# Releasing the steps of a woven encoder kernel by an in-kernel model of engine and tile times instead of fixed pauses

## The chip, the cores and the metric

The kernel runs on one core of one Trainium2 chip. Its time is the device time of one execution, in microseconds (us). Three runs of the kernel before gave 2302.92 to 2304.68 us, median 2303.62 us. The profiled execution has a time of its own, given with the profile below.

The engines have these names in the profile: PE is TensorE's matmul stream and PEld its weight loads, DVE is VectorE, ACT is ScalarE, POOL is GpSimd, SP is SyncE, whose queue issues most DMAs here.

## What is computed

The reference is one inference step of a two-layer encoder for 1024 prompt frames and 32 sample frames, with a model width of 1024. Layer 0 mixes with a matrix memory (mLSTM), layer 1 with sliding-window attention. Each is followed by a SwiGLU block, and each sub-layer ends in a layer norm of `alpha * x + sublayer(x)`:

```python
def layer_norm(x, g, b):
    mu = jnp.mean(xf, -1, keepdims=True)
    var = jnp.mean(jnp.square(xf - mu), -1, keepdims=True)
    return (xf - mu) * lax.rsqrt(var + LN_EPS) * g + b

def swiglu(x, w_gu, w_down):                  # D_FF = 2816
    g, u = jnp.split(x @ w_gu, 2, axis=-1)
    return (jax.nn.silu(g) * u) @ w_down

# mLSTM, per chunk and head; C is the matrix memory, n its normaliser
num = w_inter[..., None] * (q @ C0) + (q @ k.T * d) @ v
den = w_inter * (q @ n0) + sum(q @ k.T * d, -1)
h = num / jnp.maximum(jnp.abs(den), jnp.exp(-m))[..., None]
C_new = decay * C0 + einsum('bhs,bhsd,bhse->bhde', w_end, k, v)

# attention with a sink, 16 query heads on 2 shared key/value heads of 64
s = q @ k.T * HEAD_DIM ** -0.5 + bias         # own chunk of 64 and the two before
p = exp(s - mx) / (sum(exp(s - mx), -1) + exp(sink - mx))
o = p @ v

for layer in range(2):                        # trunk
    x = layer_norm(alpha * x + mixer[layer](x))
    x = layer_norm(alpha * x + swiglu(x))
```

It is done once for the prompt and once for the sample, and it also returns the updated memory states and the last keys and values.

## The kernel before, in words

The 1056 frames are the columns of every product; the 1024 features lie on partitions as 8 tiles of 128. Columns are worked in three groups (`GRP`: 384, 384, 288) or four quarters of 264.

**Dense products.** Every fp32 product is three matmuls on fp32r parts: high by high, high by low, low by high. `gemm` (L346) issues them as lines L358, L359, L360. A *low half* is the difference between a value and its rounded high half. It is one subtraction on DVE or POOL after a cast on ACT: for weights L198 and L200 (`wr` is the raw tile, `wh` and `wl` its halves, `ex` and `oh` halves kept elsewhere), for activations L388 and L389, in a layer norm L460 and L466, for attention weights L1627 and L1628.

**SwiGLU.** The blocks use a seven-product scheme of sums of blocks (banks `A` and `B`). The hidden values are staged to DRAM by `stage` and its `put` (L1139 cast, L1140 low half, then a store to `hs_*`) and loaded again by `feed` and `load`.

**The order of work around the change.** The program is one list that Python writes; each engine runs its own part of it in order, and semaphores hold an instruction whose inputs are late. What is not dense work is written as generators ("tasks"): the layer norm (`ln_task`), the matrix memory, attention, the staging, the reloads. `Weave.tick(us)` is called after each three matmuls of `gemm` with their nominal time; it counts down every task's pause, and a task whose pause is over writes its next instructions and yields the next pause. So the pauses (`GAP_M`, `GAP_A`, `LN_PACE`, `RUSH`, `FEED_W` 1.7, `FEED` 2.0, 5.2 in `stage`) fix how many dense matmuls lie on PE between two steps of a task. `pipeline` drives the items of the matrix memory (36: 4 head pairs by 9 chunks of 128 or 32 frames) and of attention (72: 8 head pairs by 9 chunks) through stages with a lag of an item between them. Which engine takes a low half is fixed: `on_vector` for weights, alternation elsewhere.

**A matrix memory item** is: scores `S` (L846), the mask product `p` on DVE (L850), values `H` (L862, L864) and the new state `T` (L867), a norm in small DVE and ACT steps (`small`, from L873), `ht` (L906), two transposes `T` (L913), a copy to `act` (L915).

**An attention item** is: scores of two heads `psS` (L1580, L1581), a fused bias and minimum on DVE (L1586), exp on ACT (L1598), a reciprocal on DVE (L1602), two scalings by it on POOL (L1604), four transposes `T` (L1624), high half on ACT and low half on DVE (L1627, L1628), values `O` (L1639, L1640), a copy and two additions to `act` (L1648, L1650).

**A layer norm of a quarter** is: two statistics matmuls `ln` (L418), four differences and squares, sums of squares (L427), two more statistics matmuls (L432), scale (ACT, DVE), and per pair of tiles a multiplication, ACT scalings, a high half (L460) and a low half (L466).

## Time and profile before

| what | value |
|---|---|
| runs, median (lowest, highest) | 2303.62 us (2302.92, 2304.68) |
| profiled execution, span | 2307.5 us |
| PE busy | 2222.9 us, 96% |
| DVE, ACT, POOL busy | 1462.9, 1024.3, 1127.6 us |
| granted TensorE clock, mean | 0.989 |

The span is from the first to the last instruction of one execution, here 3.9 us longer than the median of the runs. The stages, in time: projections to about 100 us; matrix memory between projections to 360; output projection and first layer norm to 640; SwiGLU of layer 0 to 1150 and its norm to 1250; attention between dense projections to 1510, with the output projection from about 1445; its layer norm to 1640; SwiGLU of layer 1 to 2215; the last norm and the stores to 2307.5.

In the tables of windows below, a row is: start and end in us, length, then busy time and number of instructions of PE, PEld, DVE, ACT and POOL, the granted clock, the busy share of the DMA engines and what they moved in GB/s. A row of waits is: engine, output and line that waited, what it waited for, us in total, times, longest. A row of a group is: line, engine, operation, output and inputs with shapes, count, busy us, mean ns of one, then idle time before it with what ended it.

### The profile page before, as it was taken

What the parts mean: (1) busy time and instruction counts of PE and PEld (TensorE: products, weight loads), DVE (VectorE), ACT (ScalarE), POOL (GpSimd) and SP (SyncE); (2) the same over time, 40 slices, a digit from 0 to 9 for tenths busy, and PEclk for the clock granted to TensorE, in tenths of its full rate; (3) what the DMA queues carried; (4) which work ended last, traced back from release to release, by engine and by line L of the source; (5) the groups of instructions that cost most, each with busy time, mean ns of one, the idle gap of its engine ahead of it and who ended that gap; (6) DMA issues with size and microseconds to landing.
All of it is one profiled execution on the core that took longest, in us unless ns stands there. A gap on an engine that the chain in (4) does not pass through costs nothing.

```text
span 2307.5 us, 44305 instructions
## 1 busy us (share of the span) xinstructions
PE 2222.9 (96%) x17224; PEld 2171.8 (94%) x17224; DVE 1462.9 (63%) x2754; ACT 1024.3 (44%) x2300; POOL 1127.6 (49%) x1039
## 2 busy tenths in 40 slices
PE   8999999999999999999999899899999999999997
PEld 8889989999999999999998799889999999999997
DVE  4354466768666655466667677767666666456657
ACT  3343445446444444322247687746444444431124
POOL 2443332125666666454314576723766666554422
PEclk9999999999999999999999999999999999999999
DMA  4221111401443434697423110331334444398712
GB/s 144 66 58 54 53 41 47 140 19 61 144 159 140 145 138 150 210 315 248 157 79 127 52 54 21 108 115 46 99 139 149 156 150 147 115 332 268 239 60 76
DMA packets 165089, 289.71 MB, mean 126 GB/s; under 512 B 15824, under 2 KB 120840, under 8 KB 164880
## 3 DMA queue, kind: packets, MB, share of 16 engines
q1 hardware_dynamic: 160528, 282.56, 36.3%
q10 hardware_dynamic: 4352, 4.33, 0.5%
q8 instruction: 135, 2.21, 0.4%
q14 instruction: 74, 0.61, 0.1%
HBM read 203.89 MB, written 82.94 MB: 124 GB/s over the span
## 4 chain that ended last, share of the span: by engine, by line
PE 75%; DVE 9%; ACT 7%; DMA 4%; issue 3%; POOL 2%; SPq 0%; DVEq 0%; ACTq 0%; POOLq 0%
PE A L358 9%; PE A L359 9%; PE A L360 9%; PE d L358 8%; PE d L360 7%; PE d L359 7%; PE B L358 7%; PE B L359 7%; PE B L360 7%; ACT act L454 1%; PE T L1624 1%; DMA wr<-in_dn 1%; DVE z L592 1%; POOL s L1604 1%; ACT sx L460 1%
## 5 line engine op out<-in xcount | busy, mean ns | idle before, releaser
L200 POOL TENSOR_TENSOR wl_s<-wr,wh_s 128x512 fp32r<-128x512 f32 x224 | 316.2, 1432 | 241.5 <-ACT wh_s L198 177.4
L358 PE MATMUL d<-sx,wh 128*128 128x264 f32 (+2 forms) x1080 | 349.2, 323 | 8.9 <-ACT sx L388 8.9
L359 PE MATMUL d<-sx,wh 128*128 128x264 f32 (+2 forms) x1080 | 334.2, 309 | 4.4 <-POOL sx L466 3.4
L360 PE MATMUL d<-sx,wl 128*128 128x264 f32 (+2 forms) x1080 | 334.0, 309 | 3.7 <-DVE wl L200 2.9
L198 ACT CAST wh_s<-wr 128x512 fp32r<-128x512 f32 x224 | 135.5, 617 | 320.9 <-DVE wr L175 288.7
L358 PE MATMUL A<-sx,wh_s 128*128 128x264 f32 x896 | 254.6, 284 | 2.2 <-ACT z L1268 2.2
L359 PE MATMUL A<-sx,wh_s 128*128 128x264 f32 x896 | 254.2, 284 | 0.0
L360 PE MATMUL A<-sx,wl_s 128*128 128x264 f32 x896 | 254.0, 283 | 0.0
L200 POOL TENSOR_TENSOR wl<-wr,wh 128x512 fp32r<-128x512 f32 (+2 forms) x106 | 143.8, 1365 | 219.8 <-ACT wh L198 206.2
L358 PEld LDWEIGHTS d<-sx,wh 128*128 128x128 f32 x1080 | 208.8, 193 | 13.5 <-ACT sx L388 9.4
L359 PEld LDWEIGHTS d<-sx,wh 128*128 128x128 f32 x1080 | 208.6, 193 | 6.7 <-POOL sx L466 4.2
L360 PEld LDWEIGHTS d<-sx,wl 128*128 128x128 f32 x1080 | 207.9, 192 | 4.7 <-DVE wl L200 3.4
L200 POOL TENSOR_TENSOR wl_a<-wr,wh_a 128x512 fp32r<-128x512 f32 x112 | 170.4, 1528 | 52.0 <-ACT wh_a L198 43.0
L358 PE MATMUL d<-sx,ex 128*128 128x264 f32 x624 | 181.5, 291 | 4.4 <-DVE act L1067 4.4
L360 PE MATMUL d<-sx,ex 128*128 128x264 f32 x624 | 178.3, 286 | 3.0 <-DVE ex L200 3.0
L359 PE MATMUL d<-sx,ex 128*128 128x264 f32 x624 | 177.7, 285 | 0.0
L358 PEld LDWEIGHTS A<-sx,wh_s 128*128 128x128 f32 x896 | 168.4, 188 | 2.7 <-ACT z L1268 2.7
L360 PEld LDWEIGHTS A<-sx,wl_s 128*128 128x128 f32 x896 | 168.8, 188 | 0.0
L359 PEld LDWEIGHTS A<-sx,wh_s 128*128 128x128 f32 x896 | 168.4, 188 | 0.0
L1140 POOL TENSOR_TENSOR z<-z 128x528 fp32r<-128x528 f32 x76 | 105.0, 1382 | 104.0 <-issue 51.5
L1604 POOL TENSOR_SCALAR s<-s,st 128x256 f32<-128x256 f32 (+1 forms) x144 | 122.4, 862 | 50.4 <-DVE st L1602 30.7
L1139 ACT CAST z<-z 128x528 fp32r<-128x528 f32 x136 | 85.9, 631 | 94.7 <-DVE z L1152 47.4
(322 smaller groups left out, 7375.9 us busy)
## 6 DMA issues: line engine op xcount, KB each, us to landing
wr<-in_gu SPq DMA_DIRECT2D x96, 512.0 KB, 4.5
hs_x<-z SPq DMA_DIRECT2D x72, 528.0 KB, 2.8
hs_t<-z SPq DMA_DIRECT2D x64, 528.0 KB, 3.5
sx<-hs_x SPq DMA_DIRECT2D x112, 264.0 KB, 5.2
sx<-hs_t SPq DMA_DIRECT2D x64, 264.0 KB, 5.8
ex<-hs_t SPq DMA_DIRECT2D x64, 264.0 KB, 6.6
wr<-in_dn SPq DMA_DIRECT2D x32, 512.0 KB, 6.4
ex<-hs_x SPq DMA_DIRECT2D x32, 264.0 KB, 5.7
```

The source lines that it names most:

```text
L198: self.nc.scalar.copy(hi, r)
L200: eng.tensor_sub(lo, r, hi.bitcast(F32))
L358: nc.tensor.matmul(out, ah, bh, start=start and k == 0, stop=False, **kw)
L359: nc.tensor.matmul(out, ah, bl, start=False, stop=False, **kw)
L360: nc.tensor.matmul(out, al, bh, start=False, stop=stop and k == last, **kw)
L454: nc.scalar.activation(z, z, AF.Identity, scale=gk, bias=bk)
L460: nc.scalar.copy(s2(0, kk), z2(kk))
L592: nc.vector.tensor_add(acc, acc if i > 3 else pair[1], pair[0])
L1139: nc.scalar.copy(hi.bitcast(F32R), buf(s))
L1140: eng.tensor_sub(lo.bitcast(F32R), buf(s), hi)
L1604: nc.gpsimd.tensor_scalar_mul(p[:R, h, lo:256], p[:R, h, lo:256], st[:R, 2, h : h + 1])
L1624: nc.tensor.transpose(pt[:nk, i, h, :R], p[:R, h, c : c + nk], ident[:R, :R])
```

## The change

`GAP_M`, `GAP_A`, `FEED_W`, `FEED`, `LN_PACE`, `RUSH` and `pipeline` go. A class `Clock` sees every instruction as it is written and keeps, while Python writes the program, a modelled time for each engine, for each cell of each tile, for the DMA pipe, for a lock between DVE and POOL, and for a halved TensorE clock after windows with little matmul work. A step of a task is an `At`: its engine, what it reads and writes, the buffers it needs. `Weave.tick` writes each step whose modelled start lies no later than PE's modelled time plus a lead (0.45 us; for PE steps minus 0.2 us). `Clock.sooner` gives a subtraction or addition to whichever of DVE and POOL the model ends first; it decides for weights prepared ahead (L392), `split_act`, sums, products and low halves of the layer norm (L658, L697), the staging (L1376) and the sums for the second product (L1436). `Weights.feed` becomes a task. Matrix memory and attention are written as one generator per item, and the scores of attention are released head by head. The arithmetic is the same.

```diff
+class Clock:
...
+    def begin(self, e, at):
+        held = self.lock if self.holder != e else 0.0
+        return max(self.free[e], at, held)
+
+    def sooner(self, n, *reads):
+        at = self.time(reads)
+        cost = {"DVE": 0.155 + 0.00104 * n, "Pool": 0.17 + 0.00219 * n}
+        e = min(cost, key=lambda e: self.begin(e, at) + cost[e])
+        return {"DVE": self.nc.vector, "Pool": self.nc.gpsimd}[e]
...
+            self.slow = self.window < 0 or self.busy < self.QUIET / 2
...
 class Weave:
...
-    def tick(self, us):
-        if self.feed:
-            self.feed(us)
-        for t in list(self.tasks):
-            t[1] -= us
-            while t in self.tasks and t[1] <= 0.0:
-                self._step(t)
+    def tick(self, until=0.0):
+        moved = True
+        while moved:
+            moved = False
+            for t in list(self.tasks):
+                while t in self.tasks:
+                    at = self._start(t)
+                    now = max(self.clk.now, until)
+                    if at is None or at > now + self.LEAD.get(self._engine(t), 0.45):
+                        break
+                    self._step(t)
+                    moved = True
...
         self.nc.scalar.copy(hi, r)
-        eng = self.nc.vector if key in self.on_vector else self.nc.gpsimd
+        if self.ahead:
+            eng = self.clk.sooner(w, hi)
+        else:
+            eng = self.nc.vector if key in self.on_vector else self.nc.gpsimd
         eng.tensor_sub(lo, r, hi.bitcast(F32))
...
-        us = 3 * (max(out.shape[-1], 256) / 2400.0 + 0.003)
+        wv.tick(clk.time((lhs[0][0], rhs[0][0]), (out,)))
         for k, ((ah, al), (bh, bl)) in enumerate(zip(lhs, rhs)):
...
-            wv.tick(us)
+            wv.tick()
...
             kk = s - 3
             if kk >= 0 and not final:
-                eng = nc.gpsimd if kk & 1 else nc.vector
-                eng.tensor_sub(s2(1, kk), z2(kk), s2(0, kk).bitcast(F32))
-            yield y[6]
+                yield At("EITHER", [s2(0, kk)], [s2(1, kk)])
+                clk.sooner(2 * w, s2(0, kk)).tensor_sub(s2(1, kk), z2(kk), s2(0, kk).bitcast(F32))
...
+    def attend(n, j, b):
...
+        for h in range(2):
+            yield At("Pool", [p[:R, h, lo:256], st[:R, 2]])
+            nc.gpsimd.tensor_scalar_mul(p[:R, h, lo:256], p[:R, h, lo:256], st[:R, 2, h : h + 1])
+        yield At("PE", [p[:R, :, lo:256]], room=[ring(psb, "T", 2)])
+        pt = new(psb, "T", [P, 2, 2, P], bufs=2, hold=True)
...
+        yield At("PE", lambda: [low[:], VR[:, [vi for _, _, vi in kts][-1]]], room=[ring(psb, "O", 2)], when=lambda: ast["v"] > b)
+        po = new(psb, "O", [P, 2, P], bufs=2, hold=True)
```

The order of the instructions on an engine, at three places. First PE in the matrix memory, before; `S` reads an item's keys, and the number in `p_2180` and `ht_2340` tells which item's product a row takes, the lower the earlier:

```order
L846 MATMUL S_2291<-qz_215,kT_738 128x256
L848 MATMUL T_2293<-ident,kT_738 128x128
L358 MATMUL d_2260<-wh_0_1920,sx 128x256
L359 MATMUL d_2260<-wl_0_1921,sx 128x256
L360 MATMUL d_2260<-wh_0_1920,sx 128x256
...
L862 MATMUL H_2316<-vt_739,p_2180 128x129
L864 MATMUL H_2316<-Cn_2221,qwz_217 128x129
L862 MATMUL H_2316<-vt_739,p_2180 128x129
L864 MATMUL H_2316<-Cn_2221,qwz_217 128x129
L867 MATMUL T_2317<-vt_739,ks_2182 64x129 x2
```

The change at the same kind of place, from one item's scores to its values and on to the transposes of its result:

```order
L1075 MATMUL S_2157<-qz_214,kT_740 128x256
L1077 MATMUL T_2159<-ident,kT_740 128x128
L582 MATMUL d_2140<-sx,wh_1022 128x384
L583 MATMUL d_2140<-sx,wh_1022 128x384
L584 MATMUL d_2140<-sx,wl_1023 128x384
...
L1098 MATMUL H_2179<-vt_741,p_2155 128x129
L1100 MATMUL H_2179<-Cn_2105,qwz_217 128x129
L1098 MATMUL H_2179<-vt_741,p_2155 128x129
L1100 MATMUL H_2179<-Cn_2105,qwz_217 128x129
L1102 MATMUL T_2180<-vt_741,ks_2156 64x129 x2
```

Before, the values that follow an item's scores belong to the item before it, so some 70 rows lie between the scores and the values that read them; in the change the item's own values come after six dense matmuls.

Second PE at the end of attention, before; `d` is the output projection, `T` the transposes and `O` the values of the last two items:

```order
L358 MATMUL d_17540<-sx,wh_1_17424 128x264
L359 MATMUL d_17540<-sx,wh_1_17424 128x264
L360 MATMUL d_17540<-sx,wl_1_17425 128x264
L1639 MATMUL O_17625<-hi_17583,VR 128x256
L1640 MATMUL O_17625<-lo_17584,VR 128x256
L1639 MATMUL O_17625<-hi_17583,VR 128x256
L1640 MATMUL O_17625<-lo_17584,VR 128x256
L358 MATMUL d_17643<-sx,wh_0_17430 128x264
L359 MATMUL d_17643<-sx,wh_0_17430 128x264
L360 MATMUL d_17643<-sx,wl_0_17431 128x264
L1639 MATMUL O_17651<-hi_17609,VR 128x2x32
L1640 MATMUL O_17651<-lo_17610,VR 128x2x32
```

The same place in the change:

```order
L1837 MATMUL psS_13972<-KH_13974,Q_17004 32x160
L1838 MATMUL psS_13972<-KL_13976,Q_17004 32x160
L1856 MATMUL T_17730<-ident,s_17692 128x128 x4
L1856 MATMUL T_17738<-ident,s_17710 128x32 x2
L1856 MATMUL T_17738<-ident,s_17710 32x32 x2
L1872 MATMUL O_17751<-hi_17736,VR 128x256
L1873 MATMUL O_17751<-lo_17743,VR 128x256
L1872 MATMUL O_17751<-hi_17736,VR 128x256
L1873 MATMUL O_17751<-lo_17743,VR 128x256
L1872 MATMUL O_17756<-hi_17745,VR 128x2x32
L1873 MATMUL O_17756<-lo_17748,VR 128x2x32
```

Before, dense rows stand between the steps of the last items; in the change the last scores, transposes and values follow each other with no dense row between.

Third POOL in the first layer norm, before; `z` is a sum of squares, `sx` a low half of the norm's result, `wl` one of the next weights:

```order
L427 TENSOR_TENSOR z_4632<-z_4632 128x2x264
L466 TENSOR_TENSOR sx<-act,sx 128x2x264 x2
L427 TENSOR_TENSOR z_4632<-z_4632 128x2x264
L466 TENSOR_TENSOR sx<-act,sx 128x2x264 x2
L200 TENSOR_TENSOR wl_0_5723<-wr_4964,wh_0_5722 128x512
L427 TENSOR_TENSOR z_4632<-z_4632 128x2x264
L200 TENSOR_TENSOR wl_0_5782<-wr_5021,wh_0_5781 128x512
L466 TENSOR_TENSOR sx<-act,sx 128x2x264 x2
```

The change:

```order
L658 TENSOR_TENSOR z_4632<-z_4632 128x2x264
L697 TENSOR_TENSOR sx<-act,sx 128x2x264
L658 TENSOR_TENSOR z_4632<-z_4632 128x2x264
L697 TENSOR_TENSOR sx<-act,sx 128x2x264
L392 TENSOR_TENSOR wl_6550<-wr_6316,wh_6549 128x512
L392 TENSOR_TENSOR wl_6555<-wr_6316,wh_6554 128x512
```

Fewer low halves of the norm stay on POOL; the others are on DVE. Over the whole program the count of instructions is the same on PE, and 247 subtractions and additions of two tiles move from POOL (761, now 514) to DVE (1827, now 2074): 122 low halves of weights, 76 of the staging, 22 of the layer norms, 16 of the sums for the second product, 10 sums of squares and one other.

867 lines of the change are left out of this document (521 added, 346 removed).

## The prediction

> **What bounds the kernel now.** I read the page first, then the clock of the core, then windows by stage, then PE's waits stage by stage.
>
> ```profile
> span 2307.5 us, 44305 instructions
> PE 2222.9 (96%) x17224; PEld 2171.8 (94%) x17224; DVE 1462.9 (63%) x2754; ACT 1024.3 (44%) x2300; POOL 1127.6 (49%) x1039
> core 0: 2307.5 us, clock 0.989
> ```
>
> PE is the bound: 96% of the span. The matmuls stay the same, so the change can win only what PE loses: 2307.5 - 2222.9 = 84.6 us idle, and (1 - 0.989) x 2307.5 = 25.4 us to a lower clock, which hides inside the busy time. The stages share this as follows.
>
> ```profile
> 0.00:100.00 100.00, 90.05 (x586) 86.11 (x587) 37.85 (x79) 37.56 (x86) 26.17 (x46) 0.95 0.31 105
> 100.00:360.00 260.00, 249.49 (x1783) 227.28 (x1783) 139.69 (x542) 108.90 (x387) 104.24 (x201) 0.99 0.19 54
> 360.00:640.00 280.00, 269.85 (x2074) 267.19 (x2073) 192.17 (x276) 139.94 (x266) 109.41 (x76) 0.99 0.25 85
> 640.00:1150.00 510.00, 507.54 (x4167) 507.14 (x4166) 313.33 (x380) 176.68 (x315) 285.62 (x205) 1.00 0.55 187
> 1150.00:1250.00 100.00, 97.30 (x698) 94.59 (x697) 71.54 (x120) 53.38 (x101) 25.40 (x22) 1.00 0.29 95
> 1250.00:1445.00 195.00, 180.67 (x1272) 170.66 (x1270) 145.30 (x554) 148.39 (x458) 133.08 (x166) 0.98 0.18 54
> 1445.00:1510.00 65.00, 54.56 (x396) 51.21 (x395) 52.70 (x146) 45.09 (x125) 45.29 (x43) 0.92 0.42 143
> 1510.00:1640.00 130.00, 123.18 (x966) 120.87 (x965) 92.12 (x131) 73.07 (x131) 49.02 (x33) 0.99 0.17 57
> 1640.00:2215.00 575.00, 572.16 (x4707) 571.55 (x4706) 358.98 (x426) 207.45 (x371) 330.20 (x236) 1.00 0.53 180
> 2215.00:2307.50 92.50, 78.11 (x597) 75.16 (x595) 59.25 (x105) 33.88 (x63) 19.15 (x17) 0.96 0.19 65
> ```
>
> Length less PE busy gives, in this order, 10.0, 10.5, 10.2, 2.5, 2.7, 14.3, 10.4, 6.8, 2.8 and 14.4 us. Both SwiGLU blocks, 1085 us, lose 5.3 us together: nothing can be won there. The 24.3 us before the first products and in the last stores hang on the first loads, the last norm and the stores. What can be won lies in five stages with 10.5 + 10.2 + 2.7 + 24.7 + 6.8 = 54.9 us. PE's waits say for what (the first row of the whole run, then single stages: 100 to 360, 360 to 640, 1250 to 1445, 1445 to 1510):
>
> ```profile
> PE d L358 <- ACT sx L388: 8.9, 3, 5.9
> ...
> PE T L913 <- DVE small L873: 3.1, 2, 1.9
> PE T L867 <- DVE act L915: 2.3, 4, 1.0
> PE T L913 <- DVE ks L853: 2.0, 2, 1.5
> PE S L846 <- DVE p L850: 1.9, 1, 1.9
> PE T L913 <- DVE ht L906: 1.1, 1, 1.1
> ...
> PE d L358 <- DVE act L1067: 4.4, 1, 4.4
> PE d L359 <- POOL sx L466: 1.7, 1, 1.7
> PE d L360 <- DVE wl L200: 1.5, 1, 1.5
> ...
> PE psS L1580 <- DVE st L1586: 5.5, 3, 3.1
> PE psS L1580 <- DVE Q L1498: 2.6, 3, 1.3
> ...
> PE T L1624 <- DVE st L1602: 2.7, 2, 1.5
> PE ln L418 <- DVE z L592: 2.2, 1, 2.2
> ```
>
> These are few waits, one to four each, not one per item: a step released too early stands in PE's queue with ready dense work behind it. A pause that is right for most items is wrong for some, which is what a release by a modelled time addresses.
>
> **The change, part by part.**
>
> *Matrix memory (100 to 360).* Its five rows of waits add to 10.4 us, all that PE loses there. Each is a task's step that came too early. In the change I counted dense rows between a step and its reader: some 70 rows lie between scores and their values before, six at the place shown now. With the durations of these rows the mean cover falls from 7.8 to 4.1 us for scores to values and from 8.5 to 7.3 us for values to transposes (estimates from the order). The new covers are shorter, but each is set where the model says that the input is ready. I leave 2 us: -8.
>
> *Output projection and first norm (360 to 640).* The wait of 4.4 us is behind a DMA: one load of x, ahead of four weight loads on SP's queue.
>
> ```profile
> 402.82 0.59 SPq L1041 DMA_DIRECT2D act<-in_x  x1
> 403.58 14.64 SPq L157 DMA_DIRECT2D wr<-in_wout_a  x4
> ```
>
> The order on SP is the same in the change, but the four loads are written some 7 us of PE's work later, no longer right behind x, and by the order and their 3 to 4 us each they land at least 4 us before PE reads them (estimates); so the wait of 4.4 us should go. The low halves of the norm on POOL are the second reason:
>
> ```profile
> L466 POOL TENSOR_TENSOR sx<-act,sx 128x528 fp32r<-128x528 f32 x24 | 32.8, 1369 | 116.9 <-ACT sx L460 115.7 <-PE d L359 0.7 <-DMA scrx<-act 0.4
> L1271 DVE TENSOR_TENSOR z<-z,B 128x528 f32<-128x528 f32 x40 | 28.1, 702 | 74.0 <-PE B L360 74.0
> ```
>
> 22 of the 24 move to DVE; a subtraction of the same size takes 1369 ns on POOL and about 702 ns on DVE, 0.67 us less on the way to the next product. Of the 10.2 us I leave 3: -7. The same answer at the second norm (6.8 us, same two kinds of wait) is -4, and -1.5 for 1150 to 1250 with the SwiGLU blocks.
>
> *Attention (1250 to 1445).* 31 of the 38 weight low halves that POOL does here move to DVE.
>
> ```profile
> L1604 POOL TENSOR_SCALAR s<-s,st 128x256 f32<-128x256 f32 x112 | 102.2, 925 | 42.8 <-DVE st L1602 27.9 <-PE psS L1581 7.8 <-PE T L1624 3.5
> L200 POOL TENSOR_TENSOR wl<-wr,wh 128x512 fp32r<-128x512 f32 x38 | 49.7, 1317 | 23.0 <-ACT wh L198 20.2 <-PE O L1639 2.1 <-PE d L359 0.7
> L1627 ACT CAST hi<-T 128x512 fp32r<-128x512 f32 x56 | 32.9, 587 | 27.6 <-PE T L1624 27.0
> L1628 DVE TENSOR_TENSOR lo<-T,hi 128x512 fp32r<-128x512 f32 x56 | 38.7, 691 | 12.2 <-ACT hi L1627 11.1
> ```
>
> POOL's scalings no longer stand behind a 1317 ns subtraction. DVE pays 31 x 0.69 = 21 us: its 145.3 + 52.7 = 198 us of 260 become 219, against 235 us of PE. So DVE has room on the mean, but little, and every item passes through it several times. Mean cover from the second scores to the transposes rises from 6.1 to 7.2 us, and from transposes to values falls from 3.6 to 2.4 us, where the two halves alone need 0.59 + 0.69 = 1.3 us. Steady stretches of this stage already lose little, its start a lot:
>
> ```profile
> 1290.00:1315.00 25.00, 21.19 (x133) 19.57 (x133) 16.55 (x61) 16.80 (x52) 15.59 (x18) 0.93 0.27 81
> 1390.00:1415.00 25.00, 24.59 (x179) 23.65 (x179) 20.03 (x78) 19.53 (x62) 17.70 (x23) 1.00 0.12 34
> ```
>
> The waits of 14.3 us are most of them for scores behind the reduction of another head (5.5) and for queries (2.6), which the release by head answers: -8.
>
> *End of attention (1445 to 1510).* Here the change writes the last scores, transposes and values without dense rows between. An item's way from scores to values is a reduction, an exponential, two scalings of 0.93 us, transposes and two halves; I estimate 5.5 to 6 us, and the last two items with the split of their outputs come to 13 to 15 us, of which some 5 us are covered by the rows left. 8.5 to 10 us stay idle, as now 10.4: -1.
>
> *Start and last norm.* No row there hangs on a release: 0. The sum of idle time is -8 - 7 - 4 - 1.5 - 8 - 1 = -29.5 us.
>
> *Clock.* The clock falls to half after a stretch of 3.41 us in which PE was partly idle:
>
> ```profile
> 1481.72:1485.13 3.41, 1.79 (x14) 1.49 (x12) 2.61 (x11) 3.36 (x10) 2.29 (x3) 1.00 0.00 0
> 1485.13:1488.54 3.41, 3.08 (x14) 2.98 (x14) 2.69 (x8) 2.26 (x8) 3.41 (x4) 0.50 0.45 121
> 420.17:423.59 3.42, 0.00 (x0) 0.00 (x0) 3.42 (x6) 3.42 (x9) 1.46 (x1) 1.00 0.27 74
> ```
>
> A half-clock stretch costs about 1.5 us of matmul time. I count 13 outside the last stores, most of the 25.4 us above. If the waits above go, I expect some 6 of them to go: -9. The Trainium skill, page "TensorE: Matmul & The Clock Gate", section "What's actually happening", says that the gate closes after at least one idle window of about 3.4 us. The first row disagrees, since PE was busy for 1.79 of 3.41 us before the half clock. By the page only the stall at 420 would count, whose half-clock stretch is the one or two that go: -3 in place of -9.
>
> *New waits.* A release set by a model has no slack: a step comes when its input should be ready, and any error of the model is a wait on PE. No row of before shows this. From below: the steady stretch above loses 0.41 us in 25, 0.016 us per us; over the 520 us of the matrix memory and attention that is 9 us. From above: the bad stretch loses 3.81 us in 25, 0.152, that is 79 us. I take 10, by the steady stretch, since most items have covers of some us.
>
> The net is -29.5 - 9 + 10 = -28.5 us, a span of 2279.0. The profiled execution is 3.9 us above the median, so the time is 2275.
>
> **The rivals.**
>
> *The model is late in each step.* Attention writes four PE steps per item, two scores, transposes, values, 288 in all. If the model thinks inputs ready 0.25 us too early on the mean, behind a DVE that is busy for 219 of 235 us, PE waits 288 x 0.25 = 72 us. For it speaks the cover of 2.4 us from transposes to values, on queues with low halves of 0.69 us ahead; against it the longer cover of scores. It decides from 28.5 / 288 = 0.10 us a step. Time: 2275 + 72 - 18 (the attention gain and the clock that would not be won) is about 2329; with half that error 2300 or so.
>
> *The waits only move.* Each wait that goes lets PE reach the next one sooner, as at the end of attention, and the clock stays: -29.5 + 28 gives 2302, no change. For it speaks that 10.4 us there stay by my own count; against it that the waits elsewhere are few and unlike each other.
>
> *Nearly all goes.* If the named waits, about 55 us of the five stages, and the 13 half-clock stretches, 20 us, all fall but for some 10 us: 2307.5 - 65, less 3.9, gives 2239. Against it the shorter covers and the end of attention.
>
> *The model does nothing more than the pauses*: the order on each engine differs in most rows, so this is excluded.
>
> **How the numbers follow.** The forecast has 0.57, its own range 2254 to 2293 by the ends of the clock and of the new waits near to it. The late model has 0.14, waits that move 0.14, nearly all gone 0.15. The time is 2275. For 8 in 10 the low end is 2240, at the rival of nearly all, the high end 2306, just above no change; the late model lies outside for the most part. About 0.2%, 4.6 us, is what a measurement can tell: faster is below 2299.0. The forecast and nearly all gone give 0.72, and 0.04 of the waits that move: faster 0.76. Same takes 0.08 of the latter and 0.01 of the late model: 0.09. Slower is 0.02 and 0.13: 0.15.
>
> **What would show it right or wrong.** Right: PE idle in 100 to 360 near 2 us and no row for `small`, `ks` or `ht` above 0.5 us; the wait for `act` after the load of x gone; the wait of scores for the reduction gone; idle time of some 9 us still at the end of attention, ahead of the last values; a mean clock of 0.993 or more. Wrong: waits for `lo` or `hi` ahead of the values in dozens; DVE's low halves of weights named as what ended PE's waits; idle time in the SwiGLU blocks above 8 us, from staging that moved to DVE. If PE's idle time is unchanged and only its places differ, the waits have moved.

## The result and the profile after

The change is slower. Its median is 2326.1 us (four runs, 2324.07 to 2327.41); runs of the kernel before taken beside it have the median 2303.49 us (2302.92 to 2304.68). The ratio is 1.0098, with the interval 1.0084 to 1.0113: 22.6 us lost where 28.6 had been forecast as won, and above the range, which ended at 2306. The ratios and intervals leave out disturbed executions; the profiled one of `mem_dma` below was such a one, so its stages are not read.

The head of the page and the clock of the core, of the change:

```profile
span 2325.6 us, 44258 instructions
PE 2239.0 (96%) x17224; PEld 2182.8 (94%) x17224; DVE 1519.5 (65%) x3001; ACT 1030.2 (44%) x2300; POOL 793.7 (34%) x792
core 0: 2325.6 us, clock 0.980
```

The span grew by 18.1 us. PE has the same 17224 instructions and is 16.1 us longer busy; its idle time is 86.6 us against 84.6. So by the page the loss is in the clock: (1 - 0.980) x 2325.6 = 46.5 us against 25.4. But that holds for the sum only, and the sum hides stages that go opposite ways. To see them I took PE's rows one by one: the interval from each to the next, less the usual interval of rows of the same kind and shape (the 40th percentile of those outside stretches of half clock). Summed over a stage this is what the stage loses, to idle time and to the clock together. The work without loss is the same 2133.5 us in every kernel here, so the columns can be compared. How the rows are grouped moves the level (by 8 us in the sum, with another grouping), but the differences between the columns by no more than about 0.5 us.

| lost, us | before | change |
|---|---|---|
| start to the first matrix memory values | 18.3 | 12.3 |
| matrix memory | 31.6 | 42.9 |
| output projection, first norm | 14.7 | 4.6 |
| SwiGLU of layer 0 | 8.2 | 6.4 |
| its norm, to the first scores | 8.0 | 4.6 |
| attention, to its last values | 46.8 | 85.1 |
| rest of the output projection, norm | 16.5 | 6.6 |
| SwiGLU of layer 1 | 6.1 | 7.3 |
| last norm | 6.5 | 2.2 |
| sum | 156.6 | 171.9 |

Five stages win 33.7 us together (6.0 + 10.1 + 3.4 + 9.9 + 4.3) and the SwiGLU blocks change by less than 2 us each; matrix memory loses 11.3 us more and attention 38.3. After PE's last row 2.5 us more pass. The windows of three stages show it; the columns are as before. Before, matrix memory, the output projection with the first norm, and attention:

```profile
95.00:347.50 252.50, 241.99 (x1746) 219.82 (x1744) 132.53 (x530) 105.01 (x377) 105.38 (x202) 0.99 0.20 56
347.50:567.10 219.60, 210.55 (x1562) 208.06 (x1563) 153.67 (x239) 114.06 (x221) 65.37 (x44) 0.99 0.21 69
1252.90:1491.20 238.30, 216.48 (x1537) 204.18 (x1537) 180.80 (x671) 181.33 (x555) 167.12 (x200) 0.97 0.19 58
```

The same stages of the change:

```profile
95.00:337.10 242.10, 223.64 (x1596) 200.16 (x1594) 124.12 (x531) 97.72 (x359) 72.54 (x172) 0.94 0.26 53
337.10:563.00 225.90, 224.44 (x1664) 222.94 (x1665) 158.25 (x296) 120.81 (x235) 5.33 (x4) 1.00 0.22 69
1248.90:1528.20 279.30, 243.19 (x1573) 223.09 (x1574) 195.76 (x702) 184.84 (x554) 132.86 (x169) 0.91 0.19 59
```

In the first norm PE is idle for 1.5 us (225.90 - 224.44) where it was for 9.1, with POOL all but empty. In attention 36 more matmuls take 41 us more: idle time goes from 21.8 to 36.1 us, and a clock of 0.91 over 279 us stands for some 25 us, against 7 at 0.97.

PE's waits of matrix memory and attention in the change (whole run, the largest of them; engine, output and line, what it waited for, us, times, longest):

```profile
PE H L1098 <- DVE p L1080: 10.3, 3, 5.7
PE psS L1837 <- DVE st L1888: 7.8, 13, 2.9
PE T L1856 <- POOL s L1851: 7.6, 14, 2.3
PE O L1872 <- DVE act L1881: 7.5, 3, 3.4
...
PE T L1162 <- DVE ht L1156: 4.6, 3, 2.6
PE O L1873 <- DVE lo L1866: 3.9, 7, 1.1
```

The waits of the norms are gone (for x, 4.4 us, and for its low half, 1.7); in their place stand waits of matrix memory values `H` and of three steps of attention. The experiments take the two stages one at a time.

### The profile page after: what moved, and what is told of

Same layout as the page of the kernel before. It is cut to its first block, busy times and chain, and to the rows that moved or that the text cites. A ratio compares the mean times of both kernels' runs of the same rounds, so it can differ in the third digit from the quotient of the medians.

```text
span 2325.6 us, 44258 instructions
## 1 busy us (share of the span) xinstructions
PE 2239.0 (96%) x17224; PEld 2182.8 (94%) x17224; DVE 1519.5 (65%) x3001; ACT 1030.2 (44%) x2300; POOL 793.7 (34%) x792
## 4 chain that ended last, share of the span: by engine, by line
PE 78%; DVE 8%; ACT 6%; DMA 4%; issue 3%; POOL 1%; SPq 0%; ACTq 0%; POOLq 0%; DVEq 0%
PE d L582 9%; PE d L583 9%; PE d L584 9%; PE A L582 8%; PE A L584 8%; PE A L583 8%; PE B L582 6%; PE B L583 6%; PE B L584 6%; PE ln L642 1%; PE T L1856 1%; PE H L1098 1%; ACT wh L387 1%; DMA hs_x<-z 1%; PE H L1100 1%
## 5 line engine op out<-in xcount | busy, mean ns | idle before, releaser
L392 POOL TENSOR_TENSOR wl<-wr,wh 128x512 fp32r<-128x512 f32 x406 | 574.2, 1430 | 915.7 <-ACT wh L387 831.9
L387 ACT CAST wh<-wr 128x512 fp32r<-128x512 f32 (+1 forms) x531 | 319.6, 617 | 477.0 <-DVE wr L361 264.7
L582 PE MATMUL A<-sx,wh 128*128 128x264 f32 x1280 | 364.5, 285 | 3.4 <-ACT z L1510 2.9
L583 PE MATMUL A<-sx,wh 128*128 128x264 f32 x1280 | 363.1, 284 | 0.0
L584 PE MATMUL A<-sx,wl 128*128 128x264 f32 x1280 | 363.1, 284 | 0.0
L582 PEld LDWEIGHTS A<-sx,wh 128*128 128x128 f32 x1280 | 240.6, 188 | 4.3 <-ACT z L1510 3.3
L584 PEld LDWEIGHTS A<-sx,wl 128*128 128x128 f32 x1280 | 241.2, 188 | 0.0
L583 PEld LDWEIGHTS A<-sx,wh 128*128 128x128 f32 x1280 | 240.7, 188 | 0.0
L582 PE MATMUL B<-ex,wh 128*128 128x264 f32 x832 | 236.5, 284 | 0.0
L583 PE MATMUL B<-ex,wh 128*128 128x264 f32 x832 | 236.0, 284 | 0.0
L584 PE MATMUL B<-ex,wl 128*128 128x264 f32 x832 | 235.8, 283 | 0.0
L582 PE MATMUL d<-sx,ex 128*128 128x264 f32 x612 | 177.3, 290 | 0.0
L584 PE MATMUL d<-sx,ex 128*128 128x264 f32 x612 | 173.7, 284 | 1.1 <-DVE ex L392 1.1
L583 PE MATMUL d<-sx,ex 128*128 128x264 f32 x612 | 173.7, 284 | 0.0
L1376 DVE TENSOR_TENSOR z<-z 128x528 fp32r<-128x528 f32 x136 | 117.9, 880 | 69.8 <-ACT z L1374 69.4
```

The costliest lines, as they stand in the source:

```text
L387: self.nc.scalar.copy(hi, r)
L392: eng.tensor_sub(lo, r, hi.bitcast(F32))
L582: nc.tensor.matmul(out, ah, bh, start=start and k == 0, stop=False, **kw)
L583: nc.tensor.matmul(out, ah, bl, start=False, stop=False, **kw)
L584: nc.tensor.matmul(out, al, bh, start=False, stop=stop and k == last, **kw)
L1376: clk.sooner(2 * N4, hi).tensor_sub(lo.bitcast(F32R), buf(s), hi)
```

## The experiments

Each ratio is against runs of the kernel before on the same chip. All kernels compute the whole.

| kernel: the change with ... | median, us | ratio to before, interval | lost in matrix memory | in attention |
|---|---|---|---|---|
| nothing else | 2326.1 | 1.0098, 1.0084 to 1.0113 | 42.9 | 85.1 |
| `att_paced`: old attention pipeline | 2293.44 | 0.995, 0.993 to 0.997 | 42.3 | 54.4 |
| `ordered_ready`: the same, PE's steps by readiness | 2317.24 | 1.0048, 1.0033 to 1.0063 | 43.1 | 68.0 |
| `one_more_item`: one item more in flight | 2314.49 | 1.0052, 1.0035 to 1.0069 | 39.3 | 76.6 |
| `lead_m12`: PE's steps 1.0 us later | 2336.25 | 1.0138, 1.0118 to 1.0158 | 40.8 | 101.4 |
| `lead_p04`: PE's steps 0.6 us earlier | 2325.58 | 1.0099, 1.0081 to 1.0117 | 40.4 | 73.3 |
| `weights_fixed`: old choice for weights | 2322.08 | 1.0077, 1.006 to 1.0094 | 36.5 | 87.0 |
| `mem_paced`: old matrix memory pipeline | 2308.44 | 1.0015, 1.0006 to 1.0025 | 38.5 | 74.0 |
| `mem_dma`: both DMA figures of the model | 2301.91 | 0.9983, 0.9974 to 0.9993 | not read | not read |
| `dma_figures`: the same kernel again | 2300.62 | 0.9984, 0.9974 to 0.9995 | 30.6 | 76.3 |
| `dma_issue`: the issue time alone | 2323.71 | 1.0079, 1.0064 to 1.0094 | 36.1 | 90.2 |
| `dma_land`: the landing time alone | 2297.82 | 0.9974, 0.9962 to 0.9986 | 31.7 | 70.7 |
| `both_paced`: both old pipelines | 2285.14 | 0.9922, 0.9904 to 0.994 | 35.4 | 52.1 |
| `both_paced_wfixed`: and old choice for weights | 2295.89 | 0.997, 0.9959 to 0.9981 | 35.9 | 56.6 |
| `both_paced_efixed`: and every old choice | 2306.1 | 1.0007, 0.9998 to 1.0017 | 37.5 | 56.8 |
| `att_paced_dma`: old attention, both DMA figures | 2281.98 | 0.9903, 0.9886 to 0.9919 | 30.4 | 55.5 |

### Attention: is it the pace, the model's errors, or the moved low halves?

The first three edits ask what loses: the release by a model, the low halves that went to DVE, or steps that the model writes a little too early. `att_paced` puts attention back under its pauses (0.46 us of dense work after each of PE's steps) and leaves all else:

```diff
+class Pause:                       # over when that much dense work is written
+    def __init__(self, wv, us):
+        self.wv, self.due = wv, wv.dense + us
...
-    def attend(n, j, b):           # one task per item
+    def attention(gap):            # one pipeline: scores, soft, turn, values, place
...
+            wv.dense += 3 * (max(out.shape[-1], 256) / 2400.0 + 0.003)
             wv.tick()
```

> The change with attention alone written as before: stages of a pipeline, one step per 0.46 us of dense work, all else (model, engine choice, matrix memory) as in the change. Theory pace (the release by readiness cuts the tie between items and dense work, dense work outruns the items to a barrier and they finish uncovered): attention loses about 41 us again instead of 77, so 2326 - 36 = about 2290 us. Theory DVE queue (weight low halves that moved to DVE hold the items): they stay on DVE here, so at most a third comes back, 2314 us or more.

`weights_fixed` undoes only the choice of the engine for weights:

```diff
-        if self.ahead:
-            eng = self.clk.sooner(w, hi)
-        else:
-            eng = self.nc.vector if key in self.on_vector else self.nc.gpsimd
+        eng = self.nc.vector if key in self.on_vector else self.nc.gpsimd
```

> The change, but the low halves of weights prepared ahead go to the engine that they had before (mostly POOL); every other choice stays by the model. Theory DVE queue: the wait from second scores to reduction (2.08 us a item in the change, 0.91 before) and from exponential to reciprocal (1.40, was 0.23) fall to near the old values and 20 to 36 us come back, 2290 to 2306 us. Theory pace: the long runs of attention rows without dense work stay, 2321 to 2331 us.

`lead_m12` writes each of PE's steps a microsecond later by the model, for the case that its inputs come late:

```diff
-    LEAD = {"PE": -0.2}
+    LEAD = {"PE": -1.2}
```

> The change with PE's lead at -1.2 instead of -0.2 us: a PE step is written only when its inputs should have been ready for 1.2 us. Theory late model (inputs come later than the model says, PE waits for them): waits shrink and 10 to 25 us come back, 2301 to 2316 us. Theory pace: items fall further behind the dense work, more of their rows are written at the barriers without dense work between, 2335 to 2350 us.

The window of the attention stage in the three, in this order:

```profile
1240.60:1478.70 238.10, 208.71 (x1471) 193.57 (x1470) 188.59 (x689) 180.86 (x554) 135.08 (x171) 0.97 0.17 54
```

```profile
1244.50:1523.20 278.70, 240.13 (x1560) 218.84 (x1559) 182.24 (x676) 185.68 (x558) 166.82 (x198) 0.91 0.19 61
```

```profile
1245.30:1538.20 292.90, 246.78 (x1560) 228.26 (x1559) 198.76 (x709) 185.06 (x558) 128.26 (x167) 0.88 0.18 58
```

The old pace brings the stage back to 238 us and 0.97, and the kernel by some 33 us, to faster than before. (How the 41 and 77 us of that expectation were counted isn't on record; by the table the stage loses 54.4, 46.8 before and 85.1 in the change.) The old choice for the weights makes DVE 13.5 us lighter in the stage and changes nothing of its length, so low halves of weights on DVE are not the main loss. It is not a full test of DVE's queue: the mean time from the second scores to the reduction fell only from 2.08 to 1.60 us, where it was 0.91 before. More slack makes the kernel 10 us worse. So it is not that the model is a little late in each step; a step that waits longer for a surer input only loses more.

What the pace did can be counted. In attention 841 of PE's rows belong to items; I counted those that lie in runs of at least 12 with no dense row between. Before there were 28, with the old pace 192 (144 of them in the last 53 us of the stage), in the change 374 in 16 runs, which took 91.3 us for 39.8 us of work. The pause counted dense work, so dense rows lay between two steps by construction. The model counts time: while a step's input isn't ready, PE gets the next dense product instead, until the dense part stands at its barrier (`ast["scored"] >= 3 * (i - 3)`, L1916: the next queries are not computed before the scores of an earlier group are written) with nothing to lay between the steps that follow. Then the steps come bare, that is with no dense row between, PE waits among them, and the clock halves: in stretches at half clock attention loses 24.7 us, against 6.4 before and 4.1 with the old pace. The same shows item by item in what lies on PE between an item's transposes and its values (all rows, by their usual intervals): the mean falls from 3.1 to 2.0 us, but the items with less than 1.3 us, which is what the two halves alone take, go from none of 72 (3 with the old pace) to 20. By dense rows alone they go from 5 (15) to 49.

The other engines show the same rule from the other side. DVE's wait for the reciprocal's input in the attention window, before and in the change:

```profile
DVE st L1602 <- ACT s L1598: 21.9, 39, 1.6
```

```profile
DVE st L1848 <- ACT s L1843: 1.5, 5, 0.4
```

Before, DVE stood in front of the reciprocal until the exponential was done; now it does other work first. That closes the gap on DVE and lengthens the way of the item: from the exponential to the reciprocal the mean is 1.40 us instead of 0.23, from the second scores to the reduction 2.08 instead of 0.91, and an item follows the one before it after 3.83 us instead of 3.19 (3.13 with the old pace).

Two more edits test this. If the chain is too long for the items in flight, one more should help; if bare steps are the cost, writing them earlier should. `one_more_item` and `lead_p04`:

```diff
-                    room=[ring(pb2, "s", 4)],
+                    room=[ring(pb2, "s", 5)],
...
-                p = new(pb2, "s", [P, 2, 257], bufs=4, hold=True)
+                p = new(pb2, "s", [P, 2, 257], bufs=5, hold=True)
...
-            yield At("SP", when=lambda: ast["scored"] == n and ast["placed"] > n - 5)
+            yield At("SP", when=lambda: ast["scored"] == n and ast["placed"] > n - 6)
```

> The change with one more attention item in flight (one more buffer for its weights, five instead of four). Some 3.75 items are in flight and one takes 14.6 us from its first score to its last value, so one ends every 3.8 us. Theory in flight (the rate of items is what bounds the stage, latency stays): one every 3.4 us at 4.3 in flight, 72 items give back 25 to 35 us, about 2295 us. Theory queue (the engines' queues hold the items): latency grows with the number in flight and at most 8 us come back, 2318 us or more.

```diff
-    LEAD = {"PE": -0.2}
+    LEAD = {"PE": 0.4}
```

> The change with PE's lead at +0.4 instead of -0.2 us: a PE step may be written 0.4 us before its inputs should be ready. By the program's order the rows written at barriers fall from 282 to 96, while the rows in long runs without dense work stay (374, now 384). If it is the barriers that cost, 15 to 25 us come back, about 2305 us; if it is the long runs, less than 8 us, 2318 us or more; by the theory late model the waits grow, 2335 us or more.

The windows of the stage, first with one item more, then with the earlier steps, and the clock of the latter:

```profile
1244.50:1515.30 270.80, 241.05 (x1573) 223.53 (x1574) 195.33 (x704) 184.57 (x554) 133.17 (x169) 0.90 0.19 61
```

```profile
1256.80:1524.20 267.40, 237.63 (x1573) 212.17 (x1573) 195.81 (x703) 182.09 (x554) 130.43 (x168) 0.96 0.20 61
core 0: 2323.6 us, clock 0.989
```

The item more gives 11.6 us, a third of what the pace gives; the items in flight rose only from 3.75 to 4.00 on the mean. The earlier steps give nothing in all (2325.58), though they bring the clock of the whole run to that of the kernel before, 0.989, and though far fewer of PE's rows stand right behind the barrier in the written program (96 against 282). Attention loses less (73.3), and most other stages more (the start 14.9 for 12.3, the first norm 7.4 for 4.6, the last 5.0 for 2.2). PE's waits of that run show why: more of them, for steps that now stand in its queue too early.

```profile
PE O L1873 <- DVE lo L1866: 6.7, 12, 2.2
PE T L1162 <- DVE ht L1156: 6.5, 10, 2.3
...
PE ln L642 <- DVE z L816: 3.3, 14, 0.5
```

The values wait 12 times for a low half where it was 7, the transposes of the matrix memory 10 times for `ht` where it was 3. So neither the clock nor the barrier by itself is the cost; one kind of loss is paid for the other. Small differences of this stage are to be read with care: edits that leave the code of attention as it is move its loss between 70.7 and 90.2 us (`dma_land`, `dma_issue`, below). The 76.6 of the item more and the 73.3 of the earlier steps lie within that; the 54.4 of the old pace and the 101.4 with more slack lie well outside.

`ordered_ready` then parts the two things that the old pipeline brings, its order of steps on ACT, DVE and POOL, and the tie to dense work. It is `att_paced`, with PE's steps released by readiness:

```diff
             item = seq[n[i]]
+            if pause:
+                yield At("PE", pause(*item))      # the reads of that step
             work(*item)
...
-            if pause:
-                yield Pause(wv, pause[item[0]])
```

> The one with attention paced (2293 us), with one edit: a step of PE in the pipeline is not released after 0.46 us of dense work but when the model says that its inputs are ready. The steps of ACT, DVE and POOL are written in the same groups as in the kernel before. Theory pace (the tie of PE's steps to dense work is what counts): the runs without dense work are as long as in the change (583 rows in runs of 12 and more, change 374, paced 192), 2318 to 2335 us. Theory queue (the order of the steps on DVE and ACT is what counts): 2288 to 2300 us.

The stage window of this run, and PE's largest wait in it, here and with the old pace:

```profile
1242.00:1487.20 245.20, 213.32 (x1418) 195.78 (x1416) 185.77 (x678) 177.35 (x538) 129.02 (x165) 0.95 0.14 43
PE psS L1871 <- DVE st L1877: 17.1, 21, 6.8
```

```profile
PE psS L1871 <- DVE st L1877: 11.1, 10, 6.2
```

Without the tie some 24 of the 33 us that the old pace had won are lost again, part of it behind this window (the rest of the output projection loses 15.4 us against 5.6). So the tie of PE's steps to dense work looks like the larger part of the gain of the pace; the time, 2317.24, lies just below what theory pace gave. Two things keep this from being a clean division. The edit releases the scores when their queries are ready and does not ask whether the reduction has freed their bank, and the wait for that is 6 us longer than with the old pace. And the count of bare rows does not carry the loss alone: it is 584 here, more than in the change, with a smaller loss. The way from the second scores to the reduction is 0.95 us here, as short as before, so a longer way through DVE is not what is lost here. The other 9 us are not settled; the order on ACT and DVE is what is left, but no run isolates it.

### Matrix memory: one number of the model

`mem_paced` puts the matrix memory back under its pauses, with a start after 5 us of dense work as before:

```diff
+GAP_M = (0.6, 1.666, 1.519, 1.5)
...
-        task = wv.launch(mlstm())
+        task = wv.launch(mlstm(GAP_M))
+        wv.launch(go())
```

> The change with the matrix memory alone written as before: pipeline stages by dense pauses, and its start held back by 5 us of dense work. Theory pace: the stall at 138 to 162 us with its 24 us of half clock goes and the stage loses 31 us instead of 43, so about 2315 us. If the loss there comes from the loads of the mask rows alone, whatever the order of the steps, less than 4 us come back, 2322 us or more.

```profile
95.00:364.40 269.40, 256.11 (x1817) 234.14 (x1815) 150.72 (x569) 110.18 (x390) 80.33 (x178) 0.98 0.21 52
```

It gives 18 us, but only 4.4 of them in its own stage, where the expectation had 12; 11.1 come in attention, whose code is the same (what the model releases there hangs on all that was written before). In its own stage the loss at half clock falls from 17.3 to some 4 us, so the stall is gone, but some 9 us more are lost elsewhere in the stage. What the stall is, the timeline of the change shows (start, duration, queue or engine, line; in brackets the idle time before and what ended it):

```profile
140.99 1.96 SPq L343 DMA_DIRECT2D wr<-in_wqk  x2
...
148.41 1.06 SPq L1042 DMA_DIRECT2D nm<-scrm  x2
...
149.84 0.39 PE L1162 MATMUL T<-ident,ht 32*128 32x32 f32 x2 [2.64 <-DVE ht L1156]
150.16 0.69 PE L582 MATMUL d<-sx,oh 128*128 128x384 f32 x1
...
158.17 0.72 POOL L1061 TENSOR_TENSOR nm<-nm,cmask 128x256 f32<-128x256 f32 x1 [11.30 <-DMA nm<-scrm]
...
160.19 1.23 PE L1098 MATMUL H<-vt,p 128*128 128x129 f32 x4 [5.71 <-DVE p L1080]
```

A mask load (`nm`, 128 KB in rows of 512 bytes) issued at 148.41 is used at 158.17, 9.8 us later, behind 1 MB of weights issued at 140.99. With nothing ahead of it the model gives it 1.3 us, then 0.66 for its bytes, then 0.7: some 2.7 us. Everything of that item is written as if the mask were there, and PE stands before `H` for 5.7 us with dense products written behind it. That is the second half of the stall. In the first, from 138.4 to 150.16 us, PE has no dense row at all: the dense part stands at its barrier here (`mst["done"] >= 9 * (j - 1)`, L1192), and the last steps of the first nine items come bare, with gaps of 1.5, 1.4, 1.3 and 2.6 us. The clock fell there, 6 us before the mask load was issued, by windows of 3.4 us (the last column, GB/s, shows that the weights' bytes too came late, most of them from 149 us on):

```profile
138.55:141.97 3.42, 0.69 (x5) 0.40 (x5) 2.79 (x9) 3.32 (x13) 1.16 (x2) 1.00 0.09 19
141.97:145.38 3.41, 2.08 (x8) 0.63 (x9) 2.69 (x11) 0.56 (x2) 0.00 (x0) 0.50 0.99 54
145.38:148.79 3.41, 1.83 (x9) 0.70 (x8) 1.27 (x8) 1.54 (x7) 0.15 (x2) 0.50 0.37 35
148.79:152.21 3.42, 2.37 (x8) 2.33 (x9) 0.99 (x5) 0.19 (x1) 0.00 (x0) 0.50 0.88 311
152.21:155.62 3.41, 2.27 (x7) 1.47 (x6) 0.00 (x0) 0.00 (x0) 0.00 (x0) 0.50 0.90 62
155.62:159.03 3.41, 0.00 (x0) 0.00 (x0) 0.00 (x0) 0.10 (x1) 0.86 (x2) 0.50 0.20 31
...
162.45:165.86 3.41, 3.41 (x11) 3.14 (x11) 0.17 (x1) 2.35 (x10) 2.09 (x5) 0.50 0.07 21
165.86:169.27 3.41, 3.41 (x25) 3.00 (x24) 1.79 (x9) 0.00 (x0) 0.58 (x2) 1.00 0.17 49
```

From 141.97 to 165.86 the clock is half, 23.9 us. In stretches at half clock matrix memory loses 17.3 us in the change and 2.5 before. So the stall is bare steps first, as in attention, and a load later than the model says after them.

Two figures of the model's DMA were then changed, first both, then each alone: what an issue takes on its queue (the two issues above took 1.06 us together, the model has 0.06 each), and 4 us more to the landing of short rows, by the wait above and no finer.

```diff
-            self.free[e] = start + 0.06
-            end = self.pipe + 0.7
+            self.free[e] = start + 0.45                              # dma_issue
+            end = self.pipe + 0.7 + (4.0 if row <= 512 else 0.0)     # dma_land
```

> The change with two figures of its model nearer to the trace: 0.45 us instead of 0.06 us for SP to issue a DMA, and 4 us more for a DMA of rows of at most 512 bytes to land (the mask rows of the matrix memory, issued at 148.4 us, were used at 158.2 us; the model had 3 us). Theory wrong load times: the waits of H for p (10.3 us) and the half clock behind them go, the matrix memory gives back 12 to 20 us, about 2310 us. Theory pace: the waits move to the next step, 2321 us or more.

The same kernel ran again as `dma_figures`, with the two single edits beside it.

> The one with the two DMA figures of the model corrected (2302 us), once more for a profile, since the first was taken in a disturbed execution. If the gain of 24 us comes from the matrix memory, its stage (about 100 to 340 us, 18 us idle and 12 us of half clock in the change) loses 15 us or more less, and attention loses about as much as in the change; if it comes from attention by chance of another order, the matrix memory is as in the change.

> Only the first figure: 0.45 us instead of 0.06 us for SP to issue a DMA. If the model's cost of issuing on SP is what mattered, about 2305 us; if the landing time of short rows is what mattered, 2320 to 2328 us.

> Only the second figure: 4 us more for a DMA of rows of at most 512 bytes to land. If the landing time of the mask rows is what mattered, about 2305 us; if the cost of issuing is, 2320 to 2328 us.

The landing time alone turns the change from 1.0098 to 0.9974, some 28 us; the issue time alone does next to nothing (1.0079), and both together are no better than the one. (`dma_figures` loses 12.3 us less in the matrix memory and 8.8 less in attention: between its two expectations.) The matrix memory window and what is left of the wait for the mask product with the landing time:

```profile
95.00:321.60 226.60, 218.51 (x1590) 196.53 (x1588) 127.19 (x529) 97.29 (x359) 74.37 (x173) 0.98 0.27 56
PE S L1075 <- DVE small L1151: 3.4, 1, 3.4
...
PE H L1098 <- DVE p L1080: 0.6, 1, 0.6
```

The 10.3 us before `H` are 0.6, idle time is 8.1 us instead of 18.5, the clock 0.98 instead of 0.94. By stages 11.2 of the 28 us are the matrix memory's, 4.1 lie before it, and 14.4 in attention. The last are the caution here: 70.7 with the landing time alone, 76.3 with both, 90.2 with the issue time, and whether the edit reaches it through its own loads or through the order of what comes before was not followed. A stage that the model drives moves by 10 to 20 us when something ahead of it changes.

The edit makes the model wait; it does not make the load faster. The first mask load of the same item with the landing time alone, then with both figures, where it stands right behind the same two weight loads:

```profile
139.82 0.38 SPq L1042 DMA_DIRECT2D nm<-scrm  x1
148.05 0.73 POOL L1061 TENSOR_TENSOR nm<-nm,cmask 128x256 f32<-128x256 f32 x1 [7.67 <-DMA nm<-scrm]
```

```profile
131.96 2.07 SPq L343 DMA_DIRECT2D wr<-in_wqk  x2
134.59 0.38 SPq L1042 DMA_DIRECT2D nm<-scrm  x1
138.48 0.72 POOL L1061 TENSOR_TENSOR nm<-nm,cmask 128x256 f32<-128x256 f32 x1 [5.36 <-DVE small L1112]
```

In the first it still takes 8.2 us, but PE waits only 0.6 us, since the item's values are written later. In the second it is used after 3.9 us, and POOL did not wait for it, though the 1 MB was issued only 2.6 us earlier. So neither the short rows nor the weights ahead are shown to be what made the load of the change slow.

### The engine that ends first

With both old pipelines the release of those two stages is out of the way, and what is left of the change can be taken apart. `both_paced` is `att_paced` and `mem_paced` together; `both_paced_wfixed` adds the edit of `weights_fixed`; `both_paced_efixed` undoes every `sooner`, so that 1827 and 761 instructions stand on DVE and POOL as before:

```diff
-        clk.sooner(GRP[g][1], sxh[k][g][:]).tensor_sub(...)
+        nc.vector.tensor_sub(...)
...
-                yield At("EITHER", [s2(0, kk)], [s2(1, kk)])
-                clk.sooner(2 * w, s2(0, kk)).tensor_sub(...)
+                e = "Pool" if kk & 1 else "DVE"
+                yield At(e, [s2(0, kk)], [s2(1, kk)])
+                ENG[e].tensor_sub(...)
```

> The change with both attention and the matrix memory written as before (pipelines of stages paced by dense work); the model still releases layer norms, staging, reloads and weights, and still chooses between DVE and POOL. Theory pace: the two gains add, 2293 - 18 = about 2276 us, faster than the kernel before by about 28 us. If the two stages only hand their waits to each other, 2288 us or more.

> As the one with both paced, and the low halves of weights prepared ahead on the engine that they had before. If the choice of the engine by the earlier modelled end is worth something once the pace is right, this is slower than the one with both paced by 5 us or more; if DVE's queue suffers from it, faster by 5 us or more; if the choice does not matter there, within 4 us.

> As the one with both paced (2285 us), and every choice between DVE and POOL undone: the subtractions and additions stand on the same engines as in the kernel before (1827 on DVE, 761 on POOL). What remains of the change is the release of norms, staging, reloads and weights by the model. If the release there is what won the 19 us against the kernel before, 2285 to 2292 us; if the engine choice won it, 2298 to 2306 us. Fixing the weights alone gave 2296 us, so I expect 2296 to 2303 us.

`both_paced` itself came out between its two expectations: on top of the old attention pipeline the old matrix memory is worth some 8 us, not 18. From the first of the three to the last the ratio goes 0.9922, 0.997, 1.0007. So the choice of the engine is worth 0.85%, some 20 us, rather more than half of it the weights. With it undone, what the model still releases (norms, staging, reloads) can't be told from the pauses in the total. By stages it can: `both_paced_efixed` loses some 8 us less than the kernel before at the start and 5, 6, 9 and 3 us less in and around the four norms, but 4 more in the SwiGLU of layer 0, 6 more in matrix memory and 10 more in attention. The same edit for the weights in the change itself moved the ratio from 1.0098 to 1.0077, the other way, and by less than the intervals tell apart.

### The two repairs together

`att_paced_dma` is `att_paced` with both DMA figures: the model keeps matrix memory, the pauses keep attention.

> Attention paced by dense work (2293 us) and the two DMA figures corrected, the matrix memory released by the model. If the gain of the DMA figures is in the matrix memory, the two add: 2293 - 20 = about 2273 us, the fastest so far; if it was in attention, 2290 us or more.

```profile
span 2278.5 us, 44273 instructions
...
core 0: 2278.5 us, clock 0.992
```

```profile
95.00:321.50 226.50, 220.34 (x1600) 197.66 (x1600) 125.19 (x529) 96.99 (x359) 74.51 (x173) 0.98 0.28 57
1225.50:1464.70 239.20, 208.81 (x1471) 193.65 (x1470) 189.17 (x690) 182.75 (x558) 135.06 (x172) 0.98 0.18 56
```

At 0.9903 it is faster than both kernels, than the one before by 23.1 us (2305.11 on the same chip), than the change by some 44. The gains don't add: 33 and 28 us apart would be 61. Of the 28 some 14 lay in attention, which the pace wins anyway: against `att_paced` the matrix memory loses 11.9 us less here and attention 1.1 us more. From `both_paced` (0.9922) it can't be told.

## Why the prediction was wrong

The terms of the sum beside what the stages lost more or less (idle time and clock together, so the term for the clock is in them):

| step | forecast, us | measured, us |
|---|---|---|
| matrix memory | -8 | +11.3 |
| output projection and first norm | -7 | -10.1 |
| SwiGLU blocks and the norm between | -1.5 | -4.0 |
| attention and its end | -8 - 1 | +38.3 |
| second norm | -4 | -9.9 |
| start, last norm | 0 | -10.3 |
| after PE's last row | 0 | +2.5 |
| clock | -9 | in the rows above; in all +21 |
| new waits | +10 | in the rows above |

**Right: the norms.** The wait for x went as the order on SP said, and POOL is out of the way: PE's waits left in that stage are two, of the statistics and the next product. The gain was larger than forecast. That the moved low halves gave it is shown only in part: with every choice of engine undone (`both_paced_efixed`) the first norm still loses 5 us less than before, against 9 less with the choices (`both_paced`).

```profile
PE d L584 <- DVE ex L392: 1.1, 1, 1.1
...
PE ln L642 <- DVE z L658: 0.4, 1, 0.4
```

The start and the last norm, set to 0, won 6.0 and 4.3 us. DVE with 247 more instructions was indeed nowhere the bound: with the old pipelines a move of 240 is worth some 20 us.

**Wrong: "each is set where the model says that the input is ready. I leave 2 us: -8" (matrix memory).** The step took the model's word for a load that the trace of before could have been asked about: there, for the mask tiles of the whole stage, stands:

```profile
DMA to landing us min/median/max: 1.7/3.3/7.3
```

The model has 2.7 us for one with nothing ahead of it, and 4 us more repaired most of the loss. The term should have been tested with the long end. With the landing time mended, the stage loses 31.7 us, as before: then still no gain of 8. The other part of the stall, the bare steps at the barrier, comes from the mistake named next, at work in this stage too.

**Wrong: "which the release by head answers: -8" (attention).** The prediction worked out what lies between two steps only as a mean over all items (its 7.2 and 2.4 us), and let the mean stand for each. The mean was about right and the spread was not looked at: between transposes and values 20 of 72 items have less than the 1.3 us that the halves take, where none had before. The pauses were read as guesses at readiness, and they were also what kept dense rows between the steps of an item. The order that was shown for the end of attention, with no dense row between the steps, was taken for the end alone; 16 such runs stand in the whole stage, whose loss went up by 38.3 us. How much of that the missing dense rows explain by themselves stays open (`ordered_ready`). The waits for the reduction that were to go went from 5.5 to 7.8 us over the whole run.

**Wrong in sign: "some 6 of them to go: -9" (clock).** It was a result of the other two steps and fell with them: 46.5 us instead of 25.4. How much of attention's loss is the half clock's own is not isolated; the earlier steps show that the clock can come back with no gain in time.

**Wrong in size: "I take 10, by the steady stretch, since most items have covers of some us" (new waits).** The upper bound of 79 us was the nearer one: matrix memory and attention together lost 49.6 us more, where the other terms, the clock aside, had 17 won, so some 67 us are left for new waits and the clock.

The rival that the model is late in each step gave 2329, close to the time, but not its mechanism. More slack on PE's steps should have cured it, and cost 10 us; waits for a half ahead of the values, its sign, were 10 (7 for `lo`, 3 for `hi`) and not dozens. It holds for the mask loads: there the model was late. That the waits only move fits `lead_p04` (2325.58 for 2326.1) and not the change itself, and nearly all going is out. Of the signs named for being right, the wait after x went, the SwiGLU blocks stayed quiet (6.5 us idle), and idle time stayed at the end of attention (13.9 us from 1460 to 1528.2); `ht` (4.6 us), idle time in matrix memory (18.5 us instead of 2) and the mean clock of 0.980 spoke against it.

## What to carry to other kernels

A pause that is counted in another stream's work does two things: it guesses when an input is ready, and it rations the work that covers the wait. A release by readiness replaces only the first, so look in the new order for steps with nothing between them, not only for steps that are too early. And a scheduler that works from a model is as good as its worst figure: compare its durations with the landings in a trace, the longest too, before trusting the order that it writes. Means over items do not show either fault; look at the spread.

## What the hardware showed that was not expected

**A load can be slow without a cause that the trace names.** The 128 KB mask load needed 9.8 us from its issue to its first use, where such loads in the kernel before landed after 3.3 us in the median and 7.3 at the longest. It stood behind 1 MB of weights that were slow themselves: from 141 to 149 us only some 0.3 MB of them moved, in packets of 4 KB that took 0.98 us in the mean (6.6 at the longest), against a median of 0.16 us in the whole run. In `dma_figures` the same 1 MB moved from 132 to 137.5 us and the mask behind it was used 3.9 us after its issue. The Trainium skill, page "DMA: Bandwidth & Descriptors", section "Anatomy of one DMA — SWDGE (gpsimd) path", gives about 2.0 us fixed plus the bytes at 436 GB/s, for another issue path than SP's; an estimate by it is 2.3 us for 128 KB alone. Neither the median nor this case agrees, and the figure that repaired the kernel is 4 us more.

**The half clock stays through busy stretches.** By the windows above it set in after a stretch with PE busy for 0.69 of 3.42 us and stayed through four stretches in a row busy for 2.08, 1.83, 2.37 and 2.27 us; here it went only after one that was busy throughout (3.41 of 3.41), elsewhere in the same run after one busy for 3.14. The Trainium skill, page "TensorE: Matmul & The Clock Gate", section "What's actually happening", has the throttled state come after an idle window of about 3.4 us; the first of these rows, like the row of before with 1.79 us, disagrees: the window need not be idle. All 12 falls of the clock in the change ahead of the last stores came after a stretch with PE busy for 0.35 to 1.73 us, none after an idle one. So stretches with PE busy for some two thirds did not bring the clock back in this run.

**Choosing the engine by the earlier end.** Moving 240 subtractions and additions from POOL to DVE, the busier of the two, was worth 0.85% where the two old pipelines set the pace (`both_paced` against `both_paced_efixed`), though DVE was busy for 189.0 of 237.3 us in the attention stage.
